# A tuned three-block transformer kernel: probabilities times values with the values stationary and two heads in the column halves of the array

## The chip, the cores and the metric

The kernel runs on one core of one Trainium2 chip. The metric is the device time of one execution in microseconds (us), as the median of three runs. Engines: TensorE (PE in the profile; its weight loads are listed apart as PEld), VectorE (DVE), ScalarE (ACT), GpSimd (POOL), and SyncE (SP), which issues the DMAs.

## The reference

One sequence of 256 tokens with 1024 channels goes through a first layer (a mixer of attention and a causal convolution, then a gated feed-forward) and a second pair of layers (feed-forward, a mixer, feed-forward; twice). Everything is float32. What the change touches is the inner part of four attentions with 8 heads of 64 channels: one in the first mixer, one in the even mixer (the one that sees only selected keys), and two in the odd mixer, which has 16 heads in two groups.

```python
s = jnp.einsum('bqhd,bkhd->bhqk', qc, kb) * scale + bias    # masked per attention
p = masked_softmax(s, valid)
return jnp.einsum('bhqk,bkhd->bqhd', p, vb)
```

The even mixer has one more attention, with 4 heads of 128 channels, whose product of probabilities and values the change leaves alone.

## The kernel before

The 256 tokens are two row tiles, t = 0 and 1, of 128 partitions. Projections keep the transposed activations stationary and move the weights, 512 columns at a time, with a split into a high and a low part, so that each product is three matmuls (lines 272 to 274). The weights stream from memory through three buffers; ScalarE makes the high part (line 242), VectorE the low part (line 243).

An attention has two steps. `scores` (line 602) makes, for each t, the products of queries and keys (line 565), whose 64 channels per head stand in one half of the rows of the array (head h in rows 64 x (h mod 2) and up). It adds the mask and takes the maximum (VectorE, line 569), makes the exponentials with their sums (ScalarE, line 572), transposes them in 128x128 blocks (TensorE, line 586) and copies these out of PSUM (ScalarE, line 589). It returns the transposed blocks and the reciprocals `rs` of the row sums, 8 numbers for each of the 128 queries. Then the values are projected and copied (`vcopy`, ScalarE, line 642). `attend` (line 613) multiplies: for each head and each block of 128 keys (one block for t = 0, two for t = 1) the transposed probabilities are stationary, 128 columns, and the 64 columns of the head's values move (line 598, `pv`). The result has queries on the partitions. VectorE multiplies it by `rs` (line 622), TensorE transposes it in four blocks (`transpose4`, line 520), and `split_T` makes the high part (ScalarE, line 509) and the low part (VectorE, line 510) for the output projection `w_out`.

In the first mixer the taps of the convolution run on TensorE at the same time (line 721), with a diagonal matrix for each tap that is loaded by DMA (`dg`, two buffers).

The order on each engine is fixed when the program is built. A planner takes instructions in program order where nothing holds them, and puts others ahead where by its estimate of times they are ready earlier; a new tile needs a free buffer. All tiles of 128x512 between the projections share one pool of 25 buffers (`slot`); a tile from it is free again after its last reader. PSUM has four banks for projections (`mm`), two for scores and products (`at`) and two for transposes (`tp`).

Of the kernel before, what the change touches and what calls it, by code (L numbers as in the profile page):

```python
# [10 lines left out]
AF = mybir.ActivationFunctionType  # L11
ALU = mybir.AluOpType
AX = mybir.AxisListType

P = 128
# [160 lines left out]
class K:  # L176
# [425 lines left out]
    def scores(self, qT, kT, mask):  # L602

        out = []
        for t in range(2):
            es, sm = self.softmax_rows(t, qT, kT, list(range(8)), mask[t] if isinstance(mask, list) else mask)
            pt = self.probs_T(t, es, list(range(8)))
            rs = self.small(8, "rs")
            self.nc.vector.reciprocal(rs, sm)
            out.append((pt, rs))  # L610
        return out

    def attend(self, sc, v):

        nc = self.nc
        res = []
        for t in range(2):
            pt, rs = sc[t]
            o = self.att()
            self.pv(t, pt, list(range(8)), v, o, 64)  # L620
            on = self.slot()
            nc.vector.tensor_tensor(
                on[:, :].rearrange("p (h d) -> p h d", d=64), o[:, :].rearrange("p (h d) -> p h d", d=64),
                rs[:, :].unsqueeze(2).broadcast_to([P, 8, 64]), op=ALU.mult)
            res.append(self.split_T(self.transpose4(on)))
        return res

    def scaled_tables(self, t, co, si, w, mul):
# [430 lines left out]
```

## Time and profile before

| what | value |
|---|---|
| median of 3 runs | 1342.89 us (1342.21 to 1345.31) |
| the profiled execution's own time | 1345.35 us |
| its span in the profile | 1343.6 us |
| mean granted TensorE clock | 0.998 of full speed |
| busy share of the span: PE, PEld, DVE, ACT, POOL | 98%, 80%, 59%, 50%, 2% |
| read from memory | 233.44 MB, 175 GB/s over the span |

The span runs from the first to the last instruction. Matmuls are pipelined: one lasts longer than the distance to the next one's start, so a busy share of 98% says that TensorE always had something under way, not that it was at its peak. The time of a stretch of matmuls is read from the starts of its rows.

### The profile page before, as it was taken

The page shows a single profiled execution, that of the slowest core. Times are in us where ns is not written, and L with a number is a line of the kernel's source. Part 1 is how long each engine was busy: PE and PEld are TensorE (multiplying, and loading weights), DVE is VectorE, ACT ScalarE, POOL GpSimd, SP SyncE. Part 2 cuts the span into 40 slices and gives each one's busy share as a digit, 9 for nine tenths or more (in the row PEclk, how much of TensorE's full clock was granted, in tenths as well). Part 3 has the DMA queues.
Part 4 walks back from the last instruction along what each step waited for, and adds up shares of the span by engine and source line. Part 5 has one row for each costly group of instructions (what it writes and reads, how often), then busy time and mean ns, then how long its engine had stood idle before and what let it go on. Part 6 is the DMA issues. An engine that isn't in the chain of part 4 may idle for free.

```text
span 1343.6 us, 16178 instructions
## 1 busy us (share of the span) xinstructions
PE 1317.5 (98%) x6226; PEld 1079.2 (80%) x6226; DVE 792.8 (59%) x1241; ACT 677.9 (50%) x1123; POOL 33.5 (2%) x47
## 2 busy tenths in 40 slices
PE   7989999999999999999999999999999999999998
PEld 5767888888888888777888888888888788888886
DVE  5987655545555547886665545655546544755543
ACT  5653644445544436755654444644435845744441
POOL 0100000000000000000000000000000000000000
PEclk9999999999999999999999999999999999999999
DMA  8652465554655554432465554655554452465540
GB/s 296 215 201 71 153 223 182 188 177 156 223 174 191 181 178 168 177 126 97 144 244 189 181 181 170 218 180 188 182 190 171 166 179 95 162 228 176 190 169 32
DMA packets 43470, 235.55 MB, mean 175 GB/s; under 512 B 4864, under 2 KB 13696, under 8 KB 16640
## 3 DMA queue, kind: packets, MB, share of 16 engines
q1 hardware_dynamic: 43392, 234.51, 50.4%
q8 instruction: 49, 0.80, 0.2%
q14 instruction: 29, 0.24, 0.1%
HBM read 233.44 MB, written 1.05 MB: 175 GB/s over the span
## 4 chain that ended last, share of the span: by engine, by line
PE 92%; DVE 3%; ACT 2%; DMA 1%; POOL 1%; issue 1%; SPq 0%; POOLq 0%; DVEq 0%; ACTq 0%
PE mm L274 28%; PE mm L272 28%; PE mm L273 28%; PE tp L382 2%; PE at L598 2%; PE at L565 1%; PE tp L520 1%; PE tp L308 1%; PE tp L586 1%; DMA dg<-dg 1%; PE mm L721 1%; ACT e L572 1%; DVE wl L243 1%; POOL qf L285 1%; DMA raw<-w 0%
## 5 line engine op out<-in xcount | busy, mean ns | idle before, releaser
L243 DVE TENSOR_TENSOR wl<-raw,wh 128x1024 fp32r<-128x1024 f32 (+2 forms) x430 | 514.3, 1209 | 410.1 <-ACT wh L242 397.7
L242 ACT ACTIVATE wh<-raw 128x1024 fp32r<-128x1024 f32 (+2 forms) x430 | 444.0, 1049 | 499.9 <-PE mm L274 469.8
L272 PE MATMUL mm<-wh,xh 128*128 128x512 f32 (+1 forms) x1168 | 458.7, 393 | 2.8 <-ACT wh L242 2.8
L273 PE MATMUL mm<-wl,xh 128*128 128x512 f32 (+1 forms) x1168 | 456.1, 391 | 0.5 <-DVE wl L243 0.5
L274 PE MATMUL mm<-wh,xl 128*128 128x512 f32 (+1 forms) x1168 | 456.6, 391 | 0.0
L272 PEld LDWEIGHTS mm<-wh,xh 128*128 128x128 f32 x1168 | 220.0, 188 | 48.4 <-ACT wh L242 3.6
L273 PEld LDWEIGHTS mm<-wl,xh 128*128 128x128 f32 x1168 | 219.9, 188 | 46.4 <-DVE wl L243 2.2
L274 PEld LDWEIGHTS mm<-wh,xl 128*128 128x128 f32 x1168 | 220.0, 188 | 44.3
L272 PE MATMUL mm<-wh,slot 128*128 128x512 f32 x536 | 210.3, 392 | 0.0
L273 PE MATMUL mm<-wl,slot 128*128 128x512 f32 x536 | 210.0, 392 | 0.0
L274 PE MATMUL mm<-wh,slot 128*128 128x512 f32 x536 | 209.7, 391 | 0.0
L272 PEld LDWEIGHTS mm<-wh,slot 128*128 128x128 f32 x536 | 100.7, 188 | 20.9 <-issue 1.0
L274 PEld LDWEIGHTS mm<-wh,slot 128*128 128x128 f32 x536 | 100.7, 188 | 20.7 <-DVE slot L510 0.2
L273 PEld LDWEIGHTS mm<-wl,slot 128*128 128x128 f32 x536 | 100.7, 188 | 20.0
L313 ACT ACTIVATE xh<-tp,cols 128x128 fp32r<-128x128 f32 x128 | 42.6, 369 | 31.0 <-PE tp L308 17.7
L314 DVE SCALAR_TENSOR_TENSOR xl<-tp,cols,xh 128x128 fp32r<-128x128 f32 x128 | 40.6, 346 | 20.5 <-ACT xh L313 19.3
L424 DVE SCALAR_TENSOR_TENSOR slot<-mm,rstd,slot 128x512 f32<-128x512 f32 (+1 forms) x60 | 41.7, 702 | 17.5 <-PE mm L274 17.5
L572 ACT ACTIVATE e<-e,mx 128x128 f32<-128x128 f32 (+1 forms) x80 | 35.3, 446 | 7.9 <-DVE mx L569 7.9
L423 ACT ACTIVATE slot<-mm,rstd 128x512 f32<-128x512 f32 (+1 forms) x60 | 36.5, 659 | 3.7 <-PE mm L274 3.7
L385 DVE TENSOR_TENSOR slot<-tp,slot 128x512 fp32r<-128x512 f32 (+1 forms) x60 | 35.9, 639 | 0.0
L337 ACT ACTIVATE junk<-mm 128x512 bf16<-128x512 f32 x24 | 14.4, 600 | 36.2 <-PE mm L274 36.2
L733 DVE SCALAR_TENSOR_TENSOR slot<-slot,cols,slot 128x256 f32<-128x256 f32 x71 | 32.2, 479 | 0.5
(115 smaller groups left out, 669.9 us busy)
## 6 DMA issues: line engine op xcount, KB each, us to landing
raw<-w SPq DMA_DIRECT2D x209, 1024.0 KB, 4.9
gb<-rows SPq DMA_DIRECT2D x7, 512.0 KB, 5.5
dg<-dg SPq DMA_DIRECT2D x11, 256.0 KB, 3.6
bias<-rev SPq DMA_DIRECT2D x2, 1024.0 KB, 7.4
raw<-w SPq DMA_DIRECT2D x2, 592.0 KB, 3.6
raw<-w SPq DMA_DIRECT2D x4, 256.0 KB, 6.2
raw<-w SPq DMA_DIRECT2D x2, 512.0 KB, 8.9
out<-xres SPq DMA_DIRECT2D x4, 256.0 KB, 2.0
```

What stands on the lines that cost most here:

```text
L242: self.nc.scalar.activation(wh[:, o], r[:, i_], AF.Copy)
L243: self.nc.vector.tensor_tensor(wl[:, o], r[:, i_], wh[:, o].bitcast(F32), op=ALU.subtract)
L272: mm(ps, xh, wh, start=start, stop=False)
L273: mm(ps, xh, wl, start=False, stop=False)
L274: mm(ps, xl, wh, start=False, stop=stop)
L313: nc.scalar.activation(xh[:, c], tp[:, j * P : (j + 1) * P], AF.Copy, scale=g)
L314: nc.vector.scalar_tensor_tensor(xl[:, c], tp[:, j * P : (j + 1) * P], g, xh[:, c].bitcast(F32), op0=ALU.mult, op1=ALU.subtract)
L385: nc.vector.tensor_tensor(hlo[:, :cw], tp, hh[:, :cw].bitcast(F32), op=ALU.subtract)
L423: nc.scalar.activation(sg[:, :cw], pg[t], AF.Silu, scale=r)
L424: nc.vector.scalar_tensor_tensor(sg[:, :cw], pu[t], r, sg[:, :cw], op0=ALU.mult, op1=ALU.mult)
L572: nc.scalar.activation(s[:, :nk], s[:, :nk], AF.Exp, bias=mx[:, h : h + 1], scale=-1.0, accum_out=sm[:, h : h + 1])
L733: nc.vector.scalar_tensor_tensor(a, hc[c][:, k : k + 256], w(c, k), a, op0=ALU.mult, op1=ALU.add)
```

## The change

The product of probabilities and values changes its roles. The values of a head (128 keys by 64 channels) become stationary, and the transposed probabilities (128 keys by 128 queries) move. The result then has channels on the partitions: even heads go to partitions 0 to 63, odd heads to 64 to 127, by placing the matmul in the first or second half of the array's columns (`tile_position`). With that it is already in the layout that the output projection takes, so the four transposes after it go. The division by the row sums, which was by partition, is now by column: in `scores` VectorE spreads the 8 reciprocals over 512 columns, four transposes on TensorE turn them, and ScalarE copies them to a tile `rr`; in `attend` the multiply takes this tile as a plain operand.

```diff
@@ scores
-            out.append((pt, rs))
+            rb, rr = self.slot(), self.slot()
+            self.nc.vector.tensor_copy(
+                rb[:, :].rearrange("p (h d) -> p h d", d=64), rs[:, :].unsqueeze(2).broadcast_to([P, 8, 64]))
+            self.nc.scalar.activation(rr, self.transpose4(rb), AF.Copy)
+            out.append((pt, rr))
@@ attend
-            pt, rs = sc[t]
+            pt, rr = sc[t]
             o = self.att()
-            self.pv(t, pt, list(range(8)), v, o, 64)
+            for h in range(8):
+                r, c = (h % 2) * 64, (h // 2) * P
+                for kb in range(t + 1):
+                    nc.tensor.matmul(
+                        o[r : r + 64, c : c + P], v[kb][:, h * 64 : (h + 1) * 64], pt[(h, kb)],
+                        start=(kb == 0), stop=(kb == t), tile_position=(0, r))
             on = self.slot()
-            nc.vector.tensor_tensor(
-                on[:, :].rearrange("p (h d) -> p h d", d=64), o[:, :].rearrange("p (h d) -> p h d", d=64),
-                rs[:, :].unsqueeze(2).broadcast_to([P, 8, 64]), op=ALU.mult)
-            res.append(self.split_T(self.transpose4(on)))
+            nc.vector.tensor_tensor(on, o, rr, op=ALU.mult)
+            res.append(self.split_T(on))
```

## Rows read from the trace of the kernel before

**Rows 1.** The page's first part: busy us (share of the span) and instructions.

```profile
PE 1317.5 (98%) x6226; PEld 1079.2 (80%) x6226; DVE 792.8 (59%) x1241; ACT 677.9 (50%) x1123; POOL 33.5 (2%) x47
```

**Rows 2.** The page's chain that ended last, by engine.

```profile
PE 92%; DVE 3%; ACT 2%; DMA 1%; POOL 1%; issue 1%; SPq 0%; POOLq 0%; DVEq 0%; ACTq 0%
```

**Rows 3.** Groups by shape on PE: operation, shapes, count, busy us, mean ns, idle.

```profile
L598 PE MATMUL at<-slot,slot 128*128 128x64 f32 x192 | 22.6, 272 | 0.0
```

**Rows 4.** Timeline of PE, odd mixer, second group: start us, duration, operation, count.

```profile
1122.05 0.39 PE L274 MATMUL mm<-wh,xl 128*128 128x512 f32 x1
1122.28 3.68 PE L598 MATMUL at<-slot,slot 128*128 128x64 f32 x32
1125.79 0.61 PE L520 MATMUL tp<-sh,slot 128*128 128x128 f32 x4
1126.24 1.90 PE L598 MATMUL at<-slot,slot 128*128 128x64 f32 x16
1127.94 0.48 PE L272 MATMUL mm<-wh,slot 128*128 128x512 f32 x1
1128.26 0.40 PE L273 MATMUL mm<-wl,slot 128*128 128x512 f32 x1
```

**Rows 5.** Timeline of PE, even mixer's first attention.

```profile
553.63 0.39 PE L273 MATMUL mm<-wl,xh 128*128 128x512 f32 x1
553.95 1.16 PE L565 MATMUL at<-slot,slot 64*128 64x128 f32 x16
555.04 0.50 PE L274 MATMUL mm<-wh,xl 128*128 128x512 f32 x1
555.38 0.40 PE L272 MATMUL mm<-wh,xh 128*128 128x512 f32 x1
...
579.98 0.60 PE L598 MATMUL at<-slot,slot 128*128 128x128 f32 x4
580.42 0.60 PE L520 MATMUL tp<-sh,slot 128*128 128x128 f32 x4
```

**Rows 6.** Timeline of PE, odd mixer, first group, scores of t = 0.

```profile
1055.06 0.71 PE L565 MATMUL at<-slot,slot 64*128 64x128 f32 x8
1055.71 0.50 PE L274 MATMUL mm<-wh,xl 128*128 128x512 f32 x1
```

**Rows 7.** Chain in order of time, first mixer: start us, us, what.

```profile
85.05 1.96 ACT e L572 x8
...
107.08 0.84 PE at L598 x8
...
117.20 0.61 PE at L598 x6
```

**Rows 8.** Groups by shape on DVE: the copy that spreads an operand, SBUF to SBUF.

```profile
L845 DVE COPY slot<-slot 128x128 f32<-128x128 f32 x2 | 0.4, 221 | 0.0
```

**Rows 9.** Timeline of ACT, even mixer, before the product.

```profile
626.48 1.07 ACT L589 ACTIVATE slot<-tp 128x512 f32<-128x512 f32 x2
627.44 1.27 ACT L642 ACTIVATE slot<-mm,rstd 128x512 f32<-128x512 f32 x2
```

**Rows 10.** Chain in order of time, odd mixer, scores of t = 1.

```profile
1062.93 1.48 ACT e L572 x6
...
1113.46 1.08 ACT e L572 x4
```

**Rows 11.** Timeline of PE, then windows (us, busy by engine, PEclk, DMA share, GB/s).

```profile
593.01 1.12 PE L862 MATMUL at<-slot,slot 32*128 32x256 f32 x4
594.07 3.32 PE L598 MATMUL at<-slot,slot 128*128 128x128 f32 x16
597.04 0.77 PE L274 MATMUL mm<-wh,xl 128*128 128x512 f32 x1
...
595.00:596.00 1.00, 1.00 (x7) 1.00 (x6) 1.00 (x4) 0.00 (x0) 0.00 (x0) 0.50 0.00 0
...
1122.00:1128.00 6.00, 6.00 (x55) 5.92 (x54) 3.74 (x4) 2.45 (x4) 0.00 (x0) 1.00 0.59 198
```

## The prediction

> **What bounds the kernel now.** I read the page first. TensorE is busy for 98% of the span, its weight loads for 80%, VectorE for 59% and ScalarE for 50% [rows 1]. The chain that ended last is 92% TensorE, with 3% VectorE and 2% ScalarE [rows 2]. So the time is the sum of what TensorE has to issue, and another engine counts only where TensorE is seen waiting for it. Next I read the instruction groups by shape, to find what the change replaces: the product of probabilities and values with 64 columns per head is line 598, 192 instructions, that is 96 products of two instructions each (a float32 product is issued twice) [rows 3]. The 272 ns of one there are no price, because each overlaps its neighbours; all prices below are distances between starts, read from the timeline. In the last attention the block runs from 1122.28 to 1127.94 us with four transposes (0.45 us) inside it: 5.66 - 0.45 = 5.21 us for 48 instructions, 0.109 us each. The next matmul then takes 0.32 us to the one after it, where a projection matmul stands 0.23 us from its neighbour, so leaving costs 0.09; entering costs nothing (1122.05 to 1122.28 is 0.23) [rows 4]. Old price of one undisturbed attention: 5.30 us. There are three like it (the one in the even mixer and the two of the odd mixer); the fourth, in the first mixer, lies among the taps of the convolution and is treated apart.
>
> What paces those 0.109 us? In the even mixer's other attention the same line moves 128 columns instead of 64, and four instructions there take 0.44 us, 0.110 each [rows 5]. Twice the moving columns cost the same, so 64 columns do not pace it: what both have in common is a load of 128 stationary columns per instruction.
>
> **The change part by part.** *The product.* The number of instructions stays at 192. Each now loads 64 stationary columns and moves 128. The trace of before has no instruction in a column half, so I bound the price from both sides. If the halves do not overlap at all, an instruction costs what 128 moving columns cost on the whole array, 0.110 us [rows 5]. If they overlap as well as can be, I take the nearest thing there is: the scores (line 565) run two heads in the two row halves. Sixteen of those with 128 moving columns last from 553.95 to 555.04, 1.09 us [rows 5]; eight of them from 1055.06 to 1055.71, 0.65 us [rows 6]. The difference is 0.44 us for eight, 0.055 each, half of 0.110: two at a time. The remainder, 0.65 - 8 x 0.055 = 0.21 us, is paid once per block. Going in costs another 0.09 (553.63 to 553.95 is 0.32 instead of 0.23) and coming out 0.11 (555.04 to 555.38) [rows 5]. So a block in halves has a fixed price of 0.41 us, against 0.09 now.
>
> The new order helps less than the scores' order: for the second 128 queries each head has four instructions in its own half before the other half gets any. If TensorE can start only in order, three of the four run alone and one beside the next head: 8 x 3 + 1 = 25 steps of twice 0.055. That gives 16 x 0.055 + 25 x 0.11 + 0.41 = 4.04 us, a saving of 1.26 per attention. If each half has its own way ahead, 48 x 0.055 + 0.41 = 3.05, a saving of 2.25. I take the middle, 1.75, since no row decides it, and for three attentions -5.3 us, with -6.8 and -3.8 as ends under overlap. Without any overlap it is 48 x 0.110 + 0.41 - 5.30 = +0.39 each, +1.2 for three.
>
> *The product in the first mixer.* There it is cut into pieces by convolution taps, and most pieces end before a wait for the taps' weights. On the chain stand only one piece of eight (0.84 us) and one of six (0.61) [rows 7]. In halves they cost 8 x 0.055 + 0.41 = 0.85 and 6 x 0.055 + 0.41 = 0.74. That is +0.1, which I put at 0. Ends: -0.6, if the pieces join and pay the 0.41 once or inside a wait; +1.0, if nothing overlaps and each piece pays 0.41 (0.8) with a little delay more. The new tiles also belong here: counting what is alive while this mixer makes its scores (4 inputs and 4 sums of the convolution, 4 of queries and keys, 6 of probabilities, 2 of values, 2 for lambda) gives 22 of 25 slots; the row sums' three make 25. A wait for a slot would stop one engine briefly; it is in the +1.0.
>
> *The transposes.* Eight groups of four (line 520) leave the attention and eight of the same shape come in behind the scores. At 0.45 us a group [rows 4] this is 3.6 us off and 3.6 on: 0 on TensorE. What they wait for is new: reciprocal, then a copy on VectorE that spreads eight numbers over 512. The nearest copy is 128 x 128 and takes 0.22 us [rows 8]; per 128x512 the ends are 0.22 and four times that, 0.88, and I take half of this, 0.44, as the operand is again a spread one. VectorE has 41% of its time free [rows 1] and takes this copy in it, so I put it at 0. Where it does not, the four transposes stand at the head of TensorE's queue with projection matmuls behind them, for at most 0.88 us a time. No line here issues a DMA, so the queues of SP and GpSimd keep what they have.
>
> *The multiply and the split.* The multiply after the product stays one instruction of 128x512. The split now reads SBUF, not PSUM, and no longer waits for transposes. All of it lies under the output projection's first half, which TensorE issues meanwhile, so I put it at 0; without that cover the way is still shorter than now by the 0.45 of the transposes. The multiply's new operand is made in the scores, a value projection ahead of its use. In the first mixer that cover is thinner (its attention is the half that is needed first), but the chain there runs on without a wait for it after the last piece [rows 7].
>
> *The copy on ScalarE.* Eight new ones of 128x512 out of PSUM. Two such copies together take 1.07 us, so one adds some 0.5 to the queue [rows 9]. Behind it stand the exponentials of the second 128 queries. In the first mixer eight of these are on the chain for 1.96 us [rows 7], in the odd mixer six for 1.48 and, in its second group, four for 1.08 [rows 10]: in these three places the copy of the first 128 queries delays TensorE by its 0.5, +1.5. In the even mixer the chain is TensorE throughout, but ScalarE goes without a break from the last probability copies to those of the values, which the product needs [rows 9]; two copies before them come to 1.0, of which I count 0.4, as output-projection matmuls are there to fill. Together +1.9. Ends: 0, if all fall into idle time, and 8 x 0.5 = 4.0.
>
> **Sum.** -5.3 + 0 + 0 + 1.9 = -3.4 us. The profiled execution took 1345.35 us, so it would become 1341.95; it lay 2.46 above the median of the runs, so the median goes from 1342.89 to 1339.5. The ends under overlap: -6.8 - 0.6 + 0 = -7.4, and -3.8 + 1.0 + 4.0 = +1.2.
>
> **Rivals.** *The halves do not overlap.* The change would then not do what it is for. Against it: row halves do overlap here [rows 5, 6]; for it: no row shows column halves, which need two moving streams over the same 128 rows. It ends on the other side: +1.2, +1.0 in the first mixer and +1.9 make +4.1, 1347.0. The point from which it decides: 3 x (48 t + 0.41 - 5.30) + 1.9 = 0 at t = 0.089 us per instruction; above that the kernel is slower.
>
> *The weight load of the second half cannot run beside the first half's matmul.* Then a load of 64 columns, by the pace above half of 0.11, adds 0.055 to the 0.110 of every instruction: 48 x 0.165 + 0.41 - 5.30 = +3.0 per attention, 9.1 for three, with the two pieces on the first mixer's chain (14 x 0.055 + 0.8 = 1.6) and 1.9 some +12.6, 1355.5. Against it: on the whole array loads are busy 80% and matmuls 98% of one span, so they do run side by side [rows 1]. The Trainium skill, page "TensorE: Matmul & The Clock Gate", Part 3, section "The mechanism", says that weight loads overlap matmuls in flight only where the row group differs; column halves share all rows, so by that rule this rival would be right. The whole-array loads of this trace speak against reading it so strictly.
>
> *ScalarE takes all back.* Every one of the eight copies stands in TensorE's way and the runs of four do not overlap: the upper end, about +1, 1344. For it: exponentials on three chains [rows 7, 10]; against: TensorE has projection matmuls to issue in all but the first mixer.
>
> *TensorE's clock falls during the new blocks.* In the even mixer it stood at 0.50 from 595 to 596, the 1.2 GHz level, after matmuls in 32 rows; sixteen instructions with 128 moving columns took 2.97 us there (594.07 to 597.04) instead of 16 x 0.110 [rows 11]. That is 1.2 us more, and with the matmuls after them, estimated at half as much again, 1.8 a fall, 7.2 for four and +3.8 in all, 1346.7. Against it: the old product's 64 moving columns leave half of each 0.109 us empty, and the clock was 1.00 throughout that block [rows 11].
>
> **How the numbers follow.** Overlap as summed: 0.60, own range 1336 to 1342. No overlap 0.24, ScalarE takes all back 0.08, clock 0.05, loads 0.03. The prediction is the first's 1339.5. The range goes from 1336.0, near the lower end under overlap, up to 1347.2, which takes in the case without overlap; outside are the loads, parts of the clock's case and the tails. Faster and slower are counted from 0.2%, 2.7 us, about what a measurement of this kernel tells from no change. With overlap -3.4 passes it in about two cases of three: 0.40. Without overlap +4.1 passes it in about two of three; with the clock and the loads: 0.25. The rest, 0.35, is the same.
>
> **What the profile after would show.** Right: line 565's 0.055 us between starts in the new product's lines, blocks near 3 to 4 us, and an unbroken pair of blocks without transposes; transposes of line 520 behind the scores; eight more ScalarE copies. Wrong: starts 0.11 apart (no overlap) or 0.16 (loads); a granted clock under 1 inside the blocks; TensorE waiting in the scores for the new copies by more than 2 us in sum; a different order elsewhere, since the issue order is planned anew for the whole program.

## The result, and the profile after

The kernel after takes 1337.27 us (median of 4 runs, 1336.56 to 1337.63), the kernel before in the same series 1342.67 (4 runs, 1342.21 to 1345.31). The ratio is 0.9947, 95% interval 0.9932 to 0.9961: faster by 5 to 9 us. The profiled execution of after took 1337.39 us, its span is 1335.6, 8.0 shorter than the span before.

The page's first line, and its chain by engine, show almost what [rows 1, 2] show:

```profile
PE 1308.6 (98%) x6226; PEld 1065.8 (80%) x6226; DVE 794.9 (60%) x1249; ACT 682.7 (51%) x1131; POOL 33.4 (3%) x47
PE 90%; DVE 4%; ACT 2%; DMA 1%; POOL 1%; issue 1%; SPq 0%; POOLq 0%; DVEq 0%; ACTq 0%
```

TensorE has as many instructions as before, VectorE and ScalarE have eight more each. TensorE is still the bound, so the place to look is again the distance between starts. The groups by shape of the new product, matmuls and weight loads (lines of the kernel after are shifted: the product is line 628, the values' copy 650, the taps 729):

```profile
L628 PE MATMUL at<-slot,slot 128*64 128x128 f32 x192 | 12.2, 276 | 1.0 <-ACT slot L650 1.0
L628 PEld LDWEIGHTS at<-slot,slot 128*64 128x64 f32 x192 | 11.0, 136 | 2.7 <-ACT slot L650 1.7 <-issue 1.0
```

Busy time fell from 22.6 us [rows 3] to 12.2, and there is one new idle time, 1.0 us behind a copy of the values on ScalarE. The timeline of PE in the odd mixer's second group, which answers to [rows 4]:

```profile
1117.31 0.39 PE L274 MATMUL mm<-wh,xl 128*128 128x512 f32 x1
1117.63 2.89 PE L628 MATMUL at<-slot,slot 128*64 128x128 f32 x48
1120.45 0.50 PE L272 MATMUL mm<-wh,slot 128*128 128x512 f32 x1
1120.79 0.39 PE L273 MATMUL mm<-wl,slot 128*128 128x512 f32 x1
```

All 48 instructions stand in one block without transposes, from 1117.63 to 1120.45: 2.82 us. Entering costs 0.09 (0.32 instead of 0.23) and leaving 0.11 (0.34). That is 3.02 against the 5.30 of before: 2.28 saved. The even mixer, PE and then ACT (the last bracket is idle time before the row, with what ended it):

```profile
626.16 0.63 PE L520 MATMUL tp<-sh,slot 128*128 128x128 f32 x4
626.54 0.47 PE L274 MATMUL mm<-wh,slot 128*128 128x512 f32 x1
628.05 2.89 PE L628 MATMUL at<-slot,slot 128*64 128x128 f32 x48 [1.03 <-ACT slot L650]
630.87 0.50 PE L272 MATMUL mm<-wh,slot 128*128 128x512 f32 x1
```

```profile
625.27 1.05 ACT L242 ACTIVATE wh<-raw 128x1024 fp32r<-128x1024 f32 x1
626.83 0.60 ACT L614 ACTIVATE slot<-tp 128x512 f32<-128x512 f32 x1 [0.50 <-PE tp L520]
627.32 1.26 ACT L650 ACTIVATE slot<-mm,rstd 128x512 f32<-128x512 f32 x2
```

Here is a wait that [rows 9] did not have. ScalarE waits 0.50 us for the transposes of the row sums, copies them, and only then copies the values; TensorE waits 1.03 us for the values.

To see in which stage the 8.0 us went, I take the time between the first residual updates behind two stages (line 329 or 350, timeline of VectorE). For the even mixer after, those are:

```profile
510.48 1.41 DVE L350 SCALAR_TENSOR_TENSOR xres<-slot,pr,xres 128x512 f32<-128x512 f32 x2
643.76 1.41 DVE L350 SCALAR_TENSOR_TENSOR xres<-slot,pr,xres 128x512 f32<-128x512 f32 x2
```

643.76 - 510.48 = 133.28. Here is the same for all kernels of this study (of the feed-forward stages, which are not in the table, the three behind the even and the odd mixer take 187.07 to 187.16 us each in all kernels, the two behind the first mixer 376.94 to 377.55 together; the first mixer counts from the span's start; "fall" says that the profiled execution shows a granted clock near 0.50 for some 3 us in that stage):

| kernel | first mixer | even mixer | odd mixer | ratio to before, 95% |
|---|---|---|---|---|
| before | 135.30 | 135.29 fall | 124.98 | 1 |
| after | 132.98 | 133.28 | 120.78 | 0.9947 (0.9932 to 0.9961) |
| e1 one half first | 134.31 | 134.68 | 123.56 | 0.9979 (0.9969 to 0.9988) |
| e2 alternate each | 133.47 | 133.19 | 120.67 | 0.9947 (0.9935 to 0.9959) |
| e3 row sums added | 134.54 | 136.64 | 127.38 | 1.0038 (1.0027 to 1.0048) |
| e4 row sums out | 138.53 two falls | 130.81 | 118.78 | 0.9938 (0.9926 to 0.9951) |
| e5 copy on VectorE | 138.21 fall | 133.44 fall | 121.47 | 0.9981 (0.9972 to 0.9990) |
| e6 first mixer only | 132.40 | 134.01 | 125.04 | 0.9986 (0.9977 to 0.9995) |
| e7 other three only | 135.58 fall | 134.60 fall | 120.96 | 0.9968 (0.9956 to 0.9981) |
| e8 even copy on VectorE | 133.08 | 132.00 | 120.78 | 0.9946 (0.9934 to 0.9959) |
| e9 three tap buffers | 133.94 fall | 134.67 fall | 121.20 | 0.9965 (0.9952 to 0.9979) |
| e10 before, three tap buffers | 135.04 fall | 133.96 | 124.99 | 1.0003 (0.9994 to 1.0012) |
| e11 one column half | 137.01 | 135.82 | 126.10 | 1.0032 (1.0019 to 1.0044) |
| e12 before, taps once | 134.69 fall | 135.38 fall | 125.02 | 0.9992 (0.9983 to 1.0001) |
| e13 taps once | 134.28 fall | 134.68 fall | 120.87 | 0.9962 (0.9950 to 0.9975) |
| e14 runs of eight | 134.09 | 133.86 | 121.90 | 0.9964 (0.9952 to 0.9977) |

From before to after the odd mixer gives 4.2 us, the even mixer 2.0 and the first mixer 2.3, of which the stretch after it takes 0.56 back (376.94 to 377.50). Of the even mixer's 2.0 about 1.3 are not the change's. The old product without a clock fall takes 134.01 and 133.96 (e6, e10), with one 135.29 and 135.38; the new one without 133.28, with one 134.67, 134.68 and 134.60. So a fall costs 1.3 to 1.4 us; before's profiled execution had one [rows 11] and after's did not. Windows of after, and below them of e9, a kernel with the same product (us, busy by engine, granted clock, DMA share, GB/s):

```profile
595.00:596.00 1.00, 1.00 (x6) 0.83 (x5) 1.00 (x3) 0.08 (x1) 0.00 (x0) 1.00 0.00 0
```

```profile
594.00:595.00 1.00, 1.00 (x6) 1.00 (x6) 1.00 (x4) 0.00 (x0) 0.00 (x0) 0.50 0.00 0
```

The first stands at 1.00, the 2.4 GHz level, the second at 0.50. Such falls are probably a part of why the median of before was 1344.1 to 1344.8 in the four later series (15 to 21 runs each), with single runs from 1342.4 to 1347.9. Of these 69 runs the 33 with a mean granted clock of 0.999 or more took 1343.7 us on average, the other 36 took 1345.4. As 1343.7 is still above the 1342.67 of the first series, falls are not all of it. I take the ratio of 0.9947, some -7 us, for the size of the change, rather than the difference of the two medians of four, -5.4.

### The profile page after: what moved, and what is told of

It reads as the page before. It is cut to its first block, busy times and chain, and to the rows that moved or that the text cites. A ratio compares the mean times of both kernels' runs of the same rounds, so it can differ in the third digit from the quotient of the medians.

```text
span 1335.6 us, 16190 instructions
## 1 busy us (share of the span) xinstructions
PE 1308.6 (98%) x6226; PEld 1065.8 (80%) x6226; DVE 794.9 (60%) x1249; ACT 682.7 (51%) x1131; POOL 33.4 (3%) x47
## 4 chain that ended last, share of the span: by engine, by line
PE 90%; DVE 4%; ACT 2%; DMA 1%; POOL 1%; issue 1%; SPq 0%; POOLq 0%; DVEq 0%; ACTq 0%
PE mm L272 27%; PE mm L274 27%; PE mm L273 27%; PE tp L382 2%; PE at L565 1%; DVE wl L243 1%; PE tp L308 1%; DMA dg<-dg 1%; PE mm L729 1%; PE tp L520 1%; PE tp L586 1%; PE at L628 1%; DVE slot L741 1%; DMA raw<-w 1%; POOL qf L285 1%
## 5 line engine op out<-in xcount | busy, mean ns | idle before, releaser
L272 PE MATMUL mm<-wh,xh 128*128 128x512 f32 (+1 forms) x1168 | 458.5, 393 | 2.5 <-ACT wh L242 2.5
L272 PEld LDWEIGHTS mm<-wh,xh 128*128 128x128 f32 x1168 | 219.9, 188 | 48.4 <-ACT wh L242 3.8
L272 PE MATMUL mm<-wh,slot 128*128 128x512 f32 x536 | 211.0, 394 | 0.0
L272 PEld LDWEIGHTS mm<-wh,slot 128*128 128x128 f32 x536 | 100.7, 188 | 21.5 <-issue 1.5
```

Source lines behind the costliest of these rows:

```text
L272: mm(ps, xh, wh, start=start, stop=False)
```

## The experiments

**Theory A:** each column half works through its own instructions side by side with the other, so a block costs 48 x 0.055 us and a fixed remainder; the row sums' part takes some of it back; the first mixer gains because other matmuls fill its waits for taps. **Rivals:** TensorE goes strictly in order (runs of four half alone); the smaller weight load, not the overlap, is the gain; the row sums' part is hidden; the first mixer gains by the product's own time.

**Where the gain stands (e6, e7).** e6 uses the new `scores` and `attend` in the first mixer alone, e7 in the other three alone.

```diff
+    def scores0(...), def attend0(...)    # as before the change
-        sc = self.scores(...)  ...  self.attend(sc, v)
+        sc = self.scores0(...) ...  self.attend0(sc, v)   # e6: even and odd; e7: first mixer
```

> Only the first mixer's attention is changed; the other three are as before. Theory A (the first mixer has a gain of its own, from fewer pieces on the chain and transposes moved under the wait for the convolution's taps): -1.5 to -2 against the kernel before, 1340.5 to 1341. Rival B (the prediction's term): 0, 1342.5.

> The even mixer's and the odd mixer's attentions are changed; the first mixer's is as before. Theory A: blocks give 3 x 2.28 = -6.8, ScalarE's copies and the split scores take 1.5 to 3 back: -4 to -5, 1337.5 to 1338.5. Rival B (the whole gain sits in these three): the changed kernel's time, 1337.2 or less.

e6 took 1342.66 us (11 runs; ratio 0.9986, 0.9977 to 0.9995), some -1.9; e7 1340.09 (0.9968, 0.9956 to 0.9981), some -4.3. The two parts add up to -6.2, within the intervals the whole. So the first mixer, which the prediction put at 0, does gain.

**What paces the product (e1, e2, e14, e11).** Three orders of the same 48 instructions, and one kernel that uses one column half only:

```diff
-            for h in range(8):
+            for h in (0, 2, 4, 6, 1, 3, 5, 7):    # e1
+            for h in (0, 2, 1, 3, 4, 6, 5, 7):    # e14
+            for h, kb in [(p + i, k) for p in range(0, 8, 2) for k in range(t + 1) for i in range(2)]:    # e2
```

```diff
-                r, c = (h % 2) * 64, (h // 2) * P
+                r, c = 0, (h // 2) * P    # e11
...
-            nc.vector.tensor_tensor(on, o, rr, op=ALU.mult)
+            nc.vector.tensor_tensor(on[:64], o[:64], rr[:64], op=ALU.mult)
+            nc.vector.tensor_tensor(on[64:], o[:64], rr[64:], op=ALU.mult)
```

> The changed kernel with the heads of the product in the order 0, 2, 4, 6, 1, 3, 5, 7: all in one half of the columns, then all in the other. Same instructions, same loads, same columns. Theory A (the gain is the two halves running side by side): an instruction costs 0.11 us again but where the halves meet; a block goes from 2.82 to about 5.3 us, three blocks +7.5, with the first mixer +8 to +9 against the changed kernel, so 1345 to 1346, slower than the kernel before. Rival B (the gain comes from the transposes that left the attention, from the new plan or from TensorE's clock): within 1 us of the changed kernel, 1337.

> The changed kernel with the halves alternating product by product for the second 128 queries, not only from head to head. The step in the prediction that took a middle between start in order and a way of its own for each half. Theory A (each half has its own way ahead already): a block stays at 2.82 us, time 1337 +- 0.7. Rival B (four in a row in one half still cost something): a block shortens by 0.2 us or more, three by 0.6 to 3, 1334.5 to 1336.5.

> The changed kernel with the heads of the product in the order 0, 2, 1, 3, 4, 6, 5, 7, so that one half gets four instructions in a row for the first 128 queries and eight for the second. Worked out with 0.11 us an instruction in its half and 0.2 us around the block. Strict order: 4.7 us for the undisturbed block. Each half about four instructions ahead: 3.3 us. No limit: 2.85 us, as in the changed kernel (2.82). The kernel's time then is 5.7, 1.4 or 0 us above the changed one's in all, for three blocks.

> The changed kernel with every head's product in the first column half, and the multiply done twice from there, so the odd heads overwrite the even ones and the output is not the reference's; the instructions and their shapes stay. Theory A (an instruction of 64 stationary and 128 moving columns costs what 128 moving columns cost on the whole array, 0.11 us, and only two halves side by side make it 0.055): the undisturbed block takes 48 x 0.11 + 0.2 = 5.5 us instead of 2.82, the even mixer and the odd mixer together are 8 us longer than in the changed kernel, and the kernel is 8 to 9 us slower than that one, 1 to 2 us slower than before. Theory B (a load of 64 columns alone makes an instruction cheaper, whichever half): the block stays under 4 us and the kernel stays faster than before.

The undisturbed block of the odd mixer's first group, timeline of PE, in e1, e2, e14 and e11 in this order (the block's start, and the next matmul's):

```profile
1071.99 4.31 PE L628 MATMUL at<-slot,slot 128*64 128x128 f32 x48
1076.23 0.50 PE L274 MATMUL mm<-wh,xl 128*128 128x512 f32 x1
```

```profile
1069.99 2.84 PE L628 MATMUL at<-slot,slot 128*64 128x128 f32 x48
1072.76 0.50 PE L274 MATMUL mm<-wh,xl 128*128 128x512 f32 x1
```

```profile
1071.12 3.44 PE L628 MATMUL at<-slot,slot 128*64 128x128 f32 x48
1074.49 0.50 PE L274 MATMUL mm<-wh,xl 128*128 128x512 f32 x1
```

```profile
1076.11 5.46 PE L628 MATMUL at<-slot,slot 128*64 128x128 f32 x48
1081.50 0.50 PE L274 MATMUL mm<-wh,xl 128*128 128x512 f32 x1
```

The blocks last 4.24, 2.77, 3.37 and 5.39 us, against 2.82 in the kernel after. e11 first: in one half an instruction costs 5.39 / 48 = 0.112 us, as much as one of 128 stationary columns moving 64 [rows 4] or 128 columns [rows 5]. The smaller load saves nothing by itself; the shorter block comes from two halves running at a time. The even and the odd mixer are 7.9 us longer than in the kernel after, where theory A had said 8. The whole kernel e11 is slower than before (1348.17 us, ratio 1.0032, some +4), as theory A said, but by more than its 1 to 2: the first mixer is 4.0 us longer than in the kernel after, which the expectation had not counted, and e11 has one multiply more in each product.

The other three tell how far a half can run ahead, if one counts in a simple model. I count each instruction as 0.11 us in its half, and let the next instruction in order start its way only when its half has fewer than n unfinished ones. Then the four orders (after, e1, e2, e14) give for n = 1: 3.63, 4.95, 2.75, 4.51 us; n = 3: 2.75, 4.29, 2.64, 3.41; n = 4: 2.64, 3.96, 2.64, 3.08; n = 5: 2.64, 3.85, 2.64, 2.97; without a limit 2.64 for all. Measured less 0.2 around the block: 2.62, 4.04, 2.57, 3.17. Of these only n = 4 fits all four within 0.1. One limit common to both halves, where an instruction starts its way only when the one five places before it is done, gives the same four numbers as n = 4; the runs do not tell these two apart. e14's 3.3 was written down from e1 with this limit, and it measured 3.37, between strict order (4.7) and no limit (2.85). In e1 I had expected almost no overlap, a block of 5.3 us and a kernel of 1345 to 1346, slower than before. It took 1342.59, still faster than before; the miss is this look ahead at the places where the halves change. e14 as a whole is some 2.3 us above the kernel after by the ratios, where 1.4 was expected; its odd mixer is 1.1 longer, two blocks' 0.55 each, and its first mixer 1.1 too, which was not expected. In the kernel the order in pairs (e2, 1337.58 us, a block 0.05 us shorter) is worth no more than the order of the change: with runs of four, four ahead is just enough.

**The row sums' part (e3, e4, e5, e8).** e3 adds it to the kernel before, unused; e4 takes it out of the kernel after; e5 moves its copy out of PSUM to VectorE in all attentions, e8 only in the even mixer.

```diff
 # e3, in the kernel before, in scores
+            rb, rr = self.slot(), self.slot()
+            self.nc.vector.tensor_copy(...)
+            self.nc.scalar.activation(rr, self.transpose4(rb), AF.Copy)
             out.append((pt, rs))
 # e4, in the kernel after: those three lines out, and in attend
-            nc.vector.tensor_tensor(on, o, rr, op=ALU.mult)
+            nc.vector.tensor_tensor(on, o, v[0], op=ALU.mult)
 # e5, and e8 with the flag of the even mixer
-            self.nc.scalar.activation(rr, self.transpose4(rb), AF.Copy)
+            self.nc.vector.tensor_copy(rr, self.transpose4(rb))
```

> The kernel before with the row sums' part added behind the scores (copy on VectorE, four transposes, copy on ScalarE), its result unused; attention's own part stays as before. Theory A (it is on TensorE's path): eight groups of transposes at 0.45 us are 3.6, and ScalarE's copies delay TensorE by 1 to 2, together +4.6 to +5.6, 1347 to 1348. Rival B (it falls into gaps): +0 to +1, 1342.5 to 1343.5.

> The changed kernel without the row sums' part: the multiply takes the first value tile as operand, so that its count and shape stay; the division by the row sums is left out. The other side of the run before. Theory A: 3.6 us of transposes and 1 to 2 us of ScalarE's delays go, 1332 to 1333. Rival B: within 1 us of the changed kernel.

> The changed kernel with the copy of the turned row sums on VectorE in place of ScalarE. Theory A (in the even mixer the product waits 1.03 us for ScalarE, whose queue has this copy ahead of the values'): that wait goes, -1, 1336.3, with up to -0.5 more where exponentials stood behind the copy in the other mixers. Rival B (VectorE's maxima for the second 128 queries then stand behind the copy): within 0.5 us of the changed kernel or +1.

> Only in the even mixer VectorE, not ScalarE, copies the row sums out of PSUM; the other three attentions keep ScalarE. Theory A (the values' copies stand behind the row-sum copy on ScalarE, and the product waits 1.03 us for them): the wait goes, the even mixer falls from 133.28 us to about 132.3, and the kernel is 0.7 to 1.0 us faster than the changed one, ratio to before about 0.994. Theory B (the wait only moves, to VectorE's chain of mask and maximum that the exponentials wait for): the even mixer stays at 133.3 or grows. In both the first mixer keeps its 132.98 and the odd mixer its 120.8, since nothing is changed there.

e3 took 1348.97 us, ratio 1.0038, some +5: theory A, the part is on TensorE's path. Its odd mixer is 2.40 longer, of which four added groups of transposes would be 4 x 0.45 = 1.8 by the price in [rows 4]; its even mixer is 2.6 longer than the old one without a fall, of which two groups would be 0.9. The waits of PE in the even mixer (from 600 to 650) name 1.0 of the rest, the same wait as in the kernel after; the other 0.7 was not separated:

```profile
PE at L598 <- ACT slot L646: 1.0, 1, 1.0
```

e4 took 1337.00 us (ratio 0.9938). Its odd mixer is 2.0 shorter than after's and its even mixer 2.5, as theory A had it, but its first mixer became 5.5 longer with another order and two clock falls, so the whole gained only little and missed theory A's 1332 to 1333. e4 is also a check of the product's price, because it has the new product and no row sums' part: against before (without a fall) its even mixer is 134.0 - 130.8 = 3.2 us shorter and its odd mixer 6.2, and 2.28 for a block with 0.9 for its two groups of transposes make 3.2 and 6.4.

e5 took 1342.75 us (ratio 0.9981): slower than after, which neither theory said. The even mixer did what was expected (133.44 with a fall, so some 132.1 without); the odd one lost 0.7 and the first mixer 5.2. e8 keeps only the part that worked. PE, ACT and DVE of its even mixer:

```profile
626.45 0.39 PE L274 MATMUL mm<-wh,slot 128*128 128x512 f32 x1
626.81 2.89 PE L631 MATMUL at<-slot,slot 128*64 128x128 f32 x48
```

```profile
625.13 1.05 ACT L242 ACTIVATE wh<-raw 128x1024 fp32r<-128x1024 f32 x1
626.08 1.25 ACT L653 ACTIVATE slot<-mm,rstd 128x512 f32<-128x512 f32 x2
```

```profile
622.80 0.43 DVE L612 COPY slot<-rs 128x512 f32<-128x512 f32 x1
625.71 0.69 DVE L615 COPY slot<-tp 128x512 f32<-128x512 f32 x1 [2.48 <-PE tp L520]
```

The values' copies follow the weights' copy at once, the product starts 0.36 us after the matmul before it, and the wait is gone. The even mixer takes 132.00, 1.28 less than in the kernel after, with the other two mixers as they were. Theory A is right here. In whole runs e8 (1336.73 us, ratio 0.9946) and the kernel after (0.9947) can't be told apart; what speaks for e8 is the profile alone. So the expected 0.7 to 1.0 us of the whole kernel is not shown.

**The first mixer (e9, e10, e12, e13).** A third buffer for the taps, and one load of four taps in place of thirteen loads, in the kernel after (e9, e13) and before (e10, e12).

```diff
-DG_BUFS = 2
+DG_BUFS = 3    # e9, e10
...
 # e12, e13: in conv_pe
-                dg = self.sl.tile(...); nc.sync.dma_start(dg, ...)
+                if "dg" not in cps:
+                    cps["dg"] = self.sl.tile(...); nc.sync.dma_start(cps["dg"], ...)
+                dg = cps["dg"]
```

> The changed kernel with three buffers for the convolution's taps instead of two, which touches only the first mixer. Theory A (what the first mixer pays after the product's pieces is waiting for the taps' DMAs, 2.6 to 5.4 us each on the chain): the waits shrink and the first mixer falls from 132.98 us by 2 to 6. Theory B (the taps' transfers share the memory's rate with the weights, so another buffer brings nothing): the first mixer stays within 1 us of 132.98.

> The kernel before with three buffers for the taps. It stands beside the run of the changed kernel with three. Theory A (the change gained its 2.3 us in the first mixer by letting other matmuls fill the waits for the taps): with the waits shorter both come closer together, the first mixers of the two then differ by under 1.3 us, and this kernel gains more by the buffer than the changed one does. Theory B (the gain is the product's own shorter time): they still differ by about 2.3.

> The kernel before, with one load of four taps in place of thirteen loads: all 50 tap products use it, so the convolution's output is not the reference's. No wait for a tap is left after the first. Theory A (the first mixer's gain of 2.3 us comes from matmuls that fill the waits for the taps): here and in the changed kernel with taps loaded once the first mixers differ by under 1 us. Theory B (it is the product's own time on TensorE, 2.3 us as in the other attentions): they differ by 2 us or more. For both the first mixer falls from 135.30 us to some 128 to 132, as 3.7 us of waits are seen on TensorE.

> The changed kernel with one load of four taps in place of thirteen, so the convolution's output is not the reference's. It stands beside the kernel before with the same edit: theory A: first mixers within 1 us of each other, and this one gains less by the edit (2.9 us of waits are there to lose) than that one; theory B: this one is 2 us or more shorter.

First what the kernel after does there, from the timeline of PE:

```profile
99.22 1.96 PE L628 MATMUL at<-slot,slot 128*64 128x128 f32 x28
102.33 3.29 PE L729 MATMUL mm<-slot,dg 128*128 128x256 f32 x14 [1.15 <-DMA dg<-dg]
105.55 1.52 PE L628 MATMUL at<-slot,slot 128*64 128x128 f32 x20
107.00 0.50 PE L272 MATMUL mm<-wh,slot 128*128 128x512 f32 x1
107.57 3.62 PE L729 MATMUL mm<-slot,dg 128*128 128x256 f32 x16
```

The product stands in two pieces and is over at 107.0; from there on matmuls of the output projection (L272 and its like) lie between the taps. In the kernel before it stood in five pieces, and the last (6 instructions, at 117.04) ended the way to the output projection's first matmul, at 117.63, after the last tap:

```profile
113.91 3.29 PE L721 MATMUL mm<-slot,dg 128*128 128x256 f32 x14 [0.66 <-DMA dg<-dg]
117.04 0.78 PE L598 MATMUL at<-slot,slot 128*128 128x64 f32 x6
117.63 0.48 PE L272 MATMUL mm<-wh,slot 128*128 128x512 f32 x1
```

With three buffers before and after differ by 1.10 us in this mixer (135.04 to 133.94), and with the taps loaded once by 0.41 (134.69 to 134.28), both pairs with a fall on either side. Theory A said under 1.3 and under 1, theory B 2 or more, so by these numbers theory A holds. The whole kernels point the same way but can't decide: with the taps loaded once the change is worth 0.9992 to 0.9962, some 4.0 us (medians 1343.87 and 1340.15), about what the other three attentions give alone in e7, and each ratio is known to 0.001, 1.3 us.

The test did not keep the two theories apart, though. All four runs also missed in size: the edits freed no 2 to 6 us, and e9 and e13 are even 1.0 and 1.3 us longer in this mixer than the kernel after, each with a fall. Without the tap waits another wait comes up at the output projection. PE in e12, then in e13 (the product's first row, the first matmul of the output projection, the matmul behind the wait):

```profile
106.53 3.68 PE L598 MATMUL at<-slot,slot 128*128 128x64 f32 x32
...
112.19 0.48 PE L272 MATMUL mm<-wh,slot 128*128 128x512 f32 x1
...
128.72 0.50 PE L272 MATMUL mm<-wh,slot 128*128 128x512 f32 x1 [2.81 <-ACT slot L509]
```

```profile
108.67 2.89 PE L628 MATMUL at<-slot,slot 128*64 128x128 f32 x48
111.49 0.33 PE L797 MATMUL tp<-sh,slot 128*128 128x128 f32 x1
111.89 0.50 PE L272 MATMUL mm<-wh,slot 128*128 128x512 f32 x1
...
128.56 0.50 PE L272 MATMUL mm<-wh,slot 128*128 128x512 f32 x1 [3.23 <-ACT slot L509]
```

The product is one block in both, 5.66 us with its transposes in e12 and 2.82 in e13. But the second half of the projection then waits for the split of the convolution's output, which the attention does not feed, and this wait ends at nearly the same time. Whatever the product saves on TensorE ahead of it becomes waiting. e9 and e10 have the same wait, of 2.8 and 2.3 us; the kernels before and after have none there. Behind it e12 and e13 show a granted clock near 0.50 from 130 to 133.

So what gives the first mixer its gain stays open. From before to after TensorE's waits for the taps fall from 3.7 to 2.8 us, which is 0.9 of the 2.3; how much of the rest is the product's own time and how much the new order was not separated. Over the runs this mixer took 132.4 to 138.5 us, also where an edit changes no instruction of TensorE in it (e5), so a lucky order is a rival for all of the 2.3.

## Why the prediction was right or wrong

Direction and range held: 1337.27 lies between 1336.0 and 1347.2. The size did not: the sum was -3.4 us, the profiled executions moved by -8.0, the ratio gives some -7. The likeliest case, overlap, was the right one. Two of its terms failed: the product in the three undisturbed attentions (put at -5.3, measured -6.8) and the product in the first mixer (put at 0, measured some -1.8). The cause is shown for the first and open for the second.

- **The product, -5.3: mis-sized.** "I take the middle, 1.75, since no row decides it" is the step that failed. The block measured 3.02 with entry and exit, where "each half has its own way ahead" had given 3.05; it saves 2.28 and not 1.75, for three blocks -6.8, which was the lower end. Runs of four need a half to be able to run about four instructions ahead, and the four orders fit that. e4 confirms the saving in two mixers.
- **The fixed price of 0.41 per block** (0.21, 0.09, 0.11), taken over from the row halves: right. 2.82 - 48 x 0.055 is 0.18, entry 0.09, exit 0.11.
- **The first mixer, 0: wrong.** It is -2.3, with 0.56 lost behind it, some -1.8; e6 confirms it with -1.9. The prediction priced the two pieces on the chain and let the others lie in waits; by the timeline only two of the five pieces (18 and 12 of 48 instructions) end before a wait for a tap. It reckoned with the order of before. In the kernel after the order is another one, a sign that the prediction itself had listed as speaking against it: the product is over at 107.0 and the output projection starts between the taps, at 107.0 and not at 117.63. That this is what shortens the mixer was argued and not shown. "If the pieces join" was seen, but only as -0.6.
- **The transposes, 3.6 off and 3.6 on:** it fits. e3 and e4 agree with 0.45 a group on TensorE's path, but neither takes the transposes apart from the rest of the row sums' part.
- **VectorE's copy, 0.44 and hidden:** the length is right, 421 ns in the group of eight, and no idle time of TensorE names it. In the first mixer it is not quite hidden: the chain of the kernel after goes over VectorE there and has this copy in it.

```profile
84.07 0.34 DVE slot L612
```

- **ScalarE's copies, +1.9:** the sum is near by luck, because the places are not right. Without the first mixer the prediction had +1.4. What is left of 2.28 per block shows that the odd mixer took back 0.36 (predicted 1.0) and the even mixer 1.5 (predicted 0.4); e4, less the transposes, gives 0.2 and 1.6. In the even mixer the wait of 1.03 for the values' copies is shown by e8, which takes it away and with it 1.28 us; the prediction had named this wait and believed that projection matmuls would fill it. The remaining 0.2 to 0.3 there was not separated.
- **The clock.** The new blocks show 1.00, so this rival did not come. But the fall that [rows 11] show was in the base of the sum: 1.3 of the 8.0 us are a fall that the profiled execution of before happened to have.

These make -6.8 - 1.8 + 1.9 = -6.7, and with the 1.3 the 8.0 of the spans. That the sum closes is no proof of its terms, since the +1.9 was found as what is left over.

**The rivals.** No overlap is excluded by 0.059 us per instruction (2.82 / 48), under the deciding 0.089; what it would have cost, e11 shows: 5.39 per block and a kernel slower than before, by the ratio some 4 us, near its +4.1. The rival of the weight loads is excluded too: by it a block would have come to 48 x 0.165 = 7.9 us. The Trainium skill, "TensorE: Matmul & The Clock Gate", Part 3, "The mechanism", lists that weight loads overlap matmuls only where the row group differs (its text also names the background weight buffer as a way ahead). Here both halves use all 128 rows, 64-column loads are busy 11.0 us beside 12.2 us of matmuls, and the measurement decides against the strict reading. "ScalarE takes all back" did not come: the row sums' part took back some 1.9 in three attentions. The clock's rival is answered above.

## What to carry to other kernels

The float32 product measured here, 64 stationary and 128 moving columns, runs nearly twice as fast when neighbours in the order use the two column halves (2.82 us against 5.39 in one half), and the order need not alternate strictly: runs of four cost 0.05 us in a block of 48 against alternating pairs (2.82 against 2.77), runs of eight 0.55 more (3.37), one half after the other 1.42 more. Where two mechanisms lie behind the ends of an estimate, their middle is a price that neither gives; choose by the mechanism, or keep both as cases. A small copy added to a busy queue costs what stands behind it: find for each new instruction the next one on its engine that TensorE needs, and move the copy there where that one is late (e8, 1.28 us of the even mixer in the profile), not everywhere (e5). A test that takes one wait away can bring up another one that hides what it was to show, as in the first mixer: look for it in the trace before reading the result.

## What was not expected of the hardware

- The column halves need not alternate: four orders of the same 48 instructions (2.82, 4.24, 2.77 and 3.37 us) fit a limit of about four unfinished instructions in a half, or of five in both.
- A float32 matmul instruction with 64 stationary columns costs the same 0.11 us in one column half as one with 128 on the whole array (5.39 us for 48, against 5.21 in [rows 4]).
- The granted clock falls to 0.50 for some 3 us at the same place of the even mixer in some kernels' profiled executions and not in others', with the same code there (after none, e9 one), and costs 1.3 to 1.4 us; before it stand matmuls in 32 rows [rows 11]; why it comes in one execution and not in the next stays open.
